# Two feed-forwards with the features of the product with w_ff1 on the partitions in seven of eight chunks

## The chip, the cores and the metric

The kernel runs on one core of a Trainium2 chip. The time is that of one execution on the device, in microseconds (us); the figure for a kernel is the median of its runs. Below, PE is TensorE (PEld its weight loads), DVE is VectorE, ACT is ScalarE, POOL is GpSimd and SP is SyncE, which issues the DMAs. "Span" is the time from the first profiled instruction of an execution to the end of the last.

## What is computed

Two transformer blocks in a row on 256 tokens of width 1024, in float32. What matters here is the feed-forward at the end of each, of width 4096 (`h` is the normalised input, (256, 1024)):

```python
# first block (pieces of hybrid_layer)
h2 = rmsnorm(x, g_ff_pre) * (1.0 + scale_f[:, None]) + shift_f[:, None]
y2 = jnp.square(jax.nn.relu(h2 @ w_ff1)) @ w_ff2
return x + gate_f[:, None] * rmsnorm(y2, g_ff_post)

# second block
h = rms_norm(x, pre_ffn_g[l])
f = jnp.square(jax.nn.relu(h @ w_ff1[l])) @ w_ff2[l]
x = x + rms_norm(f, post_ffn_g[l])
```

The rest (a gated mixer with attention, pooling and convolution in the first block; gating, attention, convolution and cross attention in the second) is as it was.

## The kernel before, in words

**Precision.** Every product is made of three matmuls in the type fp32r. A weight arrives as f32 (`raw`), ACT rounds it to `hi`, and DVE subtracts to get `lo` (`split_unit`, line 639). Activations are split in the same way (`evac_split`, line 728: ACT copies the high part, DVE subtracts for the low part). `mm3` (line 676) then adds high x high, low x high and high x low into one PSUM bank.

**Units.** Weights are loaded in units of 512 KB: two tiles of 128 rows by 512 columns. `w_ff1` and `w_ff2` have 32 units each, four to a chunk, in eight chunks of 512 features (`ffn`, line 1346). A unit takes three buffers of 128x1024 from a set of 36 (`k4`) while it is split, and two until PE has used it. A load is issued by SP when its buffer comes free.

**A chunk of the feed-forward, before.** Tokens stand on the partitions. For each of the two token tiles `t` of 128 tokens, PE holds a 128x128 tile of the transposed activations `xT[t]` as weights and moves 512 columns of `w_ff1` through: 4 units x 2 row tiles x 3 = 24 matmuls of 512 columns into the bank `f` (`chunk` and `use`, lines 833 and 681). Then `after` (line 1351): ACT takes the relu into `n` (`f1r` and `f2r` in the trace), PE transposes its four 128x128 tiles into another bank (`f1t`, `f2t`), ACT squares that (`f1s`, `f2s`), and `evac_split` makes high and low part of `r` (`f1rT`, `f2rT`), which stands with features on the partitions. The second product, with `w_ff2`, holds tiles of `r` as weights and moves 512 columns of `w_ff2`: 48 matmuls of 512 columns a chunk, added over all chunks in the four banks `y[t][i]`. The last chunk ends with `finish` for each token tile: in the first block that is `junction` (line 1369), which makes the input of the second block, in the second it writes the output.

**What feeds it.** In the first block `mixed` (line 1332) makes the activations with `norm_shift` (line 964): per token tile two halves of 512 columns, each transposed and split. In the second block `residual` and `junction` do it, quarter by quarter (`to_T_gain`). During the first chunks of the first feed-forward, DVE also adds up eight rows for the vector `GG2` (`mod_vector`), 512 KB each.

**Order.** The kernel records its operations first and plans them then. `schedule` (line 392) makes 30 passes over the list with its own costs, each pass with priorities from the one before, and takes the best. It sets the order on each engine and which buffer is used, so a change in one stage can give another order in stages behind it. An engine works in that order and waits where something is missing. Matmuls inside `rec.together()` stay together.

Of the kernel before, what the change touches and what calls it, by code (L numbers as in the profile page):

```python
# [19 lines left out]
P = 128  # L20
# [5 lines left out]
WHERE = {4: 0, 6: 1}  # L26

VERBOSE = 0
POOL_TAPS = 4
PASSES = 30  # L30
BOOST = 1.0
FADE = 0.7
# [8 lines left out]
NT = 2  # L41
# [108 lines left out]

class View:
# [57 lines left out]
class Wide:  # L209
# [367 lines left out]
def tile_two_blocks(ctx: ExitStack, tc: tile.TileContext, a: dict, out: bass.AP):  # L577
# [18 lines left out]
    def bank(name):  # L596
        return rec.tile([P, 512], "ps", name)
# [7 lines left out]
    def work(shape, tag, name, dt=F32):  # L605
        return rec.tile(shape, tag, name, dt)
# [226 lines left out]
    def chunk(wname, u0, nu, xT, name, n=512, after=None):  # L833

        us = [unit(wname, u0 + g) for g in range(nu)]
        ps = []
        for t in range(NT):
            o = bank(f"{name}{t}")
            for g in range(nu):
                use(us[g], xT[t], o[:, :n], g == 0, g == nu - 1)  # L840
            ps.append(o)
            if after:
                after(t, o)
        return ps
# [116 lines left out]
        sp.dma_start(xt, a["x"][t * P : (t + 1) * P, :])  # L961
        return xt

    def norm_shift(t, xG, r, S, name):

        hT = new_xT(f"{name}T{t}")
        for g, s in enumerate(H2):
            dve.scalar_tensor_tensor(xG[:, s], xG[:, s], r, S[:, s], op0=OP.mult, op1=OP.add)
            v = transposes(xG[:, s], 4, f"{name}{t}_t{g}")
            evac_split(hT[:, 0, 4 * g : 4 * g + 4, :], hT[:, 1, 4 * g : 4 * g + 4, :], v)  # L970
        return hT


    xrT = [work([P, 4, 256], "k4", f"xrT{h}") for h in range(2)]
# [352 lines left out]
        mT.append(m)  # L1327
    drain()
    GG1, G2, S2 = vec["GG1"], vec["G2"], vec["S2"]
    x1, hT = x0, []  # L1330

    def mixed(t, y):
        w = work([P, D], "k4", f"wG{t}")
        for s, yy in zip(H2, y):
            dve.tensor_mul(w[:, s], yy, GG1[:, s])
        r = rstd(squares(y, f"wo{t}"), f"wo{t}")
        for s in H2:
            dve.scalar_tensor_tensor(x0[t][:, s], w[:, s], r, x0[t][:, s], op0=OP.mult, op1=OP.add)
        r1 = rstd(squares([x0[t][:, s] for s in H2], f"x1{t}"), f"x1{t}")
        for s in H2:  # L1340
            dve.tensor_mul(w[:, s], x0[t][:, s], G2[:, s])
        hT.append(norm_shift(t, w, r1, S2, "h2"))

    proj("w_out", mT, "wo", mixed)

    def ffn(w1, w2, xT, name, finish):
        y = [[bank(f"{name}y{t}_{i}") for i in range(2)] for t in range(NT)]
        for c in range(8):
            rT = []

# [12 lines left out]
            for t in range(NT):
                for i in range(4):
                    use(us[i], None, y[t][i // 2], c == 0 and i % 2 == 0, c == 7 and i % 2 == 1, lambda k: (rT[t], k % 4))
                if c == 7:
                    finish(t, y[t])

    def junction(t, y, x, G, g, name):


        w = work([P, D], "k4", f"{name}w{t}")
        for s, yy in zip(H2, y):
            dve.tensor_mul(w[:, s], yy, G[:, s])
        r = rstd(squares(y, f"{name}y{t}"), f"{name}y{t}")
        hT = new_xT(f"{name}T{t}")
        for q in range(4):
            s = slice(256 * q, 256 * q + 256)
            dve.scalar_tensor_tensor(x[:, s], w[:, s], r, x[:, s], op0=OP.mult, op1=OP.add)
        to_T_gain(x, hT, g, f"{name}{t}")  # L1380
        rn = rstd(squares([x[:, s] for s in H2], f"{name}x{t}"), f"{name}x{t}")
        return hT, rn

    def residual(xs, G, g, name):
        hT, rs = [], []

        def after(t, y):
            h, r = junction(t, y, xs[t], G() if callable(G) else G, g, name)
            hT.append(h)
            rs.append(r)  # L1390

        return hT, rs, after
# [303 lines left out]
```

## Time and profile before

| | before |
|---|---|
| median of 3 runs | 812.25 us (810.99 to 816.01) |
| the profiled execution | 811.87 us, span 810.1 us |
| PE busy | 778.8 us (96%) |
| DVE busy | 583.3 us (72%) |
| ACT busy | 465.2 us (57%) |
| POOL busy | 87.8 us (11%) |
| DMA | 165.38 MB, 204 GB/s in the mean |
| granted PE clock, mean | 0.995 |

How to read it: busy time is the time in which an engine worked on at least one instruction. Matmuls are pipelined: one shows some 390 ns of duration while the next begins 227 ns after it, so the pace is read from starts, or from a piece of the chain with its count, not from the mean duration. The first feed-forward runs from some 256 to 446 us, the second from 620 us to the end.

### The profile page before, as it was taken

The numbers are of one execution on the slowest core, as the hardware profiler recorded it, in microseconds if no ns is written. First come the engines' busy times: TensorE is split into PE (matmuls) and PEld (weight loads), VectorE is DVE, ScalarE is ACT, GpSimd is POOL, SyncE is SP. The second block draws the span as 40 slices with busy tenths as digits, with TensorE's granted clock in tenths as the row PEclk, the third lists the DMA queues.
The fourth block names the chain that finished last, engine by engine and source line by source line (L and its number), as shares of the span: only waits on it lengthen the run. The fifth ranks groups of instructions, "written<-read, shape, count | busy, mean of one in ns | idle before, by whom it ended". The sixth has DMA issues, their size and how long they took to land.

```text
span 810.1 us, 10528 instructions
## 1 busy us (share of the span) xinstructions
PE 778.8 (96%) x3722; PEld 640.8 (79%) x3722; DVE 583.3 (72%) x908; ACT 465.2 (57%) x768; POOL 87.8 (11%) x133
## 2 busy tenths in 40 slices
PE   6999999999999999999999999789999999999996
PEld 4789888888877778888887887568888888888885
DVE  5998799998888985454537789999778744444513
ACT  6866665565266565455446764568567655454422
POOL 4301400004122000000000410103102100000000
PEclk9999999999999999999999999999999999999999
DMA  8999566578848775655656444033637655556501
GB/s 312 401 354 362 176 228 209 199 255 333 306 164 300 255 269 178 207 183 184 204 178 215 152 170 156 27 106 103 215 128 255 207 174 179 194 181 207 182 2 52
DMA packets 49629, 165.38 MB, mean 204 GB/s; under 512 B 5412, under 2 KB 6564, under 8 KB 49576
## 3 DMA queue, kind: packets, MB, share of 16 engines
q1 hardware_dynamic: 49576, 164.71, 58.6%
q8 instruction: 29, 0.48, 0.2%
q14 instruction: 24, 0.20, 0.1%
HBM read 163.64 MB, written 1.05 MB: 203 GB/s over the span
## 4 chain that ended last, share of the span: by engine, by line
PE 83%; DVE 7%; DMA 6%; ACT 2%; issue 1%; SPq 1%; DVEq 0%; POOLq 0%; ACTq 0%; POOL 0%
PE f2f L1645 11%; PE f2y L1645 11%; PE f1y L1645 10%; PE f1f L1645 9%; PE wo L1645 5%; PE kv L1645 3%; PE bcg L1645 3%; PE xq L1645 3%; PE bbg L1645 3%; PE xo L1645 3%; PE bag L1645 2%; DMA raw_w_xkv<-in_w_xkv_dram 2%; DVE dy L1645 2%; PE xA L1645 2%; PE aA L1645 1%; DMA raw_w_ff<-in_w_ff_dram 1%
## 5 line engine op out<-in xcount | busy, mean ns | idle before, releaser
L1645 DVE TENSOR_TENSOR lo_w_ff<-raw_w_ff,hi_w_ff 128x1024 fp32r<-128x1024 f32 x128 | 155.7, 1229 | 88.9 <-ACT hi_w_ff L1645 72.5
L1645 ACT ACTIVATE hi_w_ff<-raw_w_ff 128x1024 fp32r<-128x1024 f32 x128 | 132.8, 1056 | 83.0 <-DMA raw_w_ff<-in_w_ff_dram 70.3
L1645 DVE TENSOR_TENSOR lo_w_in<-raw_w_in,hi_w_in 128x1024 fp32r<-128x1024 f32 (+1 forms) x66 | 77.8, 1204 | 7.5 <-ACT hi_w_in L1645 6.8
L1645 PE MATMUL f1y<-hi_w_ff,f1rT 128*128 128x512 f32 x256 | 80.1, 393 | 0.2 <-DVE f1rT L1645 0.2
L1645 PE MATMUL f2f<-hi_w_ff,h5T 128*128 128x512 f32 x256 | 79.9, 393 | 0.0
L1645 PE MATMUL f2y<-hi_w_ff,f2rT 128*128 128x512 f32 x256 | 79.6, 392 | 0.0
L1645 PE MATMUL f1f<-hi_w_ff,h2T 128*128 128x512 f32 x256 | 79.6, 392 | 0.0
L1645 ACT ACTIVATE hi_w_in<-raw_w_in 128x1024 fp32r<-128x1024 f32 (+1 forms) x66 | 66.8, 1032 | 20.0 <-DMA raw_w_in<-in_w_in_dram 16.9
L1645 PEld LDWEIGHTS f2f<-hi_w_ff,h5T 128*128 128x128 f32 x256 | 47.5, 188 | 9.8 <-DVE h5T L1645 0.3
L1645 PEld LDWEIGHTS f1y<-hi_w_ff,f1rT 128*128 128x128 f32 x256 | 47.4, 188 | 10.0 <-DVE f1rT L1645 0.5
L1645 PEld LDWEIGHTS f1f<-hi_w_ff,h2T 128*128 128x128 f32 x256 | 47.6, 188 | 9.6
L1645 PEld LDWEIGHTS f2y<-hi_w_ff,f2rT 128*128 128x128 f32 x256 | 47.5, 188 | 9.4
L1645 PE MATMUL f1y<-lo_w_ff,f1rT 128*128 128x512 f32 x128 | 49.9, 390 | 0.0
L1645 PE MATMUL f2f<-lo_w_ff,h5T 128*128 128x512 f32 x128 | 49.9, 390 | 0.0
L1645 PE MATMUL f2y<-lo_w_ff,f2rT 128*128 128x512 f32 x128 | 49.9, 390 | 0.0
L1645 PE MATMUL f1f<-lo_w_ff,h2T 128*128 128x512 f32 x128 | 49.9, 390 | 0.0
L1645 PE MATMUL kv<-hi_w_xkv,memT 128*128 128x512 f32 x128 | 42.4, 412 | 6.2 <-ACT hi_w_xkv L1645 5.1
L1645 DVE TENSOR_TENSOR f1rT<-f1s,f1rT 128x512 fp32r<-128x512 f32 x16 | 11.1, 692 | 32.8 <-ACT f1rT L1645 32.8
L1645 PEld LDWEIGHTS kv<-hi_w_xkv,memT 128*128 128x128 f32 x128 | 24.4, 196 | 12.5 <-ACT hi_w_xkv L1645 5.5
L1645 DVE TENSOR_TENSOR f2rT<-f2s,f2rT 128x512 fp32r<-128x512 f32 x16 | 11.1, 692 | 30.4 <-ACT f2rT L1645 30.4
L1645 ACT ACTIVATE f2r<-f2f 128x512 f32<-128x512 f32 x16 | 9.6, 597 | 33.8 <-PE f2f L1645 33.8
L1645 PEld LDWEIGHTS f2y<-lo_w_ff,f2rT 128*128 128x128 f32 x128 | 24.0, 188 | 5.1
(461 smaller groups left out, 1729.4 us busy)
## 6 DMA issues: line engine op xcount, KB each, us to landing
raw_w_ff<-in_w_ff_dram SPq DMA_DIRECT2D x128, 512.0 KB, 3.6
raw_w_in<-in_w_in_dram SPq DMA_DIRECT2D x62, 512.0 KB, 4.6
raw_GG<-in_w_ada_dram SPq DMA_DIRECT2D x16, 512.0 KB, 5.5
raw_w_out<-in_w_out_dram SPq DMA_DIRECT2D x16, 512.0 KB, 5.2
raw_w_xkv<-in_w_xkv_dram SPq DMA_DIRECT2D x15, 512.0 KB, 9.2
G<-in_w_ada_dram SPq DMA_DIRECT2D x8, 512.0 KB, 8.1
S<-in_w_ada_dram SPq DMA_DIRECT2D x8, 512.0 KB, 9.7
raw_w_branch<-in_w_branch_dram SPq DMA_DIRECT2D x8, 512.0 KB, 4.6
```

Of the source, the lines that this page charges most:

```text
L1645: getattr(rec.real[op.eng], method)(*map(out_of, args), **{k: out_of(v) for k, v in kw.items()})
```

## The change

In chunk 0 of each feed-forward the way of before stays (`by_tokens`, the body of the old loop). Chunks 1 to 7 go through `by_features`. For each block `b` of 128 features out of the chunk's 512, PE now holds a 128x128 tile of `w_ff1` as weights, and moves activations: with the high part of the weights, both parts of all 256 tokens side by side (512 columns, into the whole bank), with the low part of the weights the high part of the activations alone (256 columns, into the bank's first half). That is 32 + 32 matmuls per chunk for the same three products. The result stands with features on the partitions. It is evacuated by block: ACT copies the bank's second half, DVE adds the first half to it, DVE takes relu and square at once (`max` and `mult`), ACT copies the high part, DVE subtracts for the low part.

For that, activations have another layout: four tiles `h2T` (or `h5T`), each with two row tiles, two parts and 256 tokens; the class `Fold` shows them to the token way as before. `rT` is laid out likewise: two tiles per chunk, each with two blocks and all 256 tokens, in place of one per token tile. `norm_shift` splits its halves in two steps of 256 columns, and so does chunk 0 with `rT`. `POOL_TAPS`, which is not used, goes. The core of the diff:

```diff
+class Fold:
+    def __init__(self, tiles, t):
+        self.tiles, self.s = tiles, slice(t * P, (t + 1) * P)
+
+    def __getitem__(self, k):
+        _, part, kt, _ = k
+        if isinstance(kt, int):
+            return self.tiles[kt // 2][:, kt % 2, part, self.s]
+        assert kt.stop - kt.start == 2 and kt.start % 2 == 0
+        return self.tiles[kt.start // 2][:, :, part, self.s]
...
+    def new_folded(name):
+        return [work([P, 2, 2, 256], "k4", f"{name}{i}", F32R) for i in range(4)]
...
-            evac_split(hT[:, 0, 4 * g : 4 * g + 4, :], hT[:, 1, 4 * g : 4 * g + 4, :], v)
+            for j in range(2):
+                k = slice(4 * g + 2 * j, 4 * g + 2 * j + 2)
+                evac_split(hT[:, 0, k, :], hT[:, 1, k, :], v[:, 2 * j : 2 * j + 2])
...
-                r = work([P, 2, 4, P], "k4", f"{name}rT{c}_{t}", F32R)
-                evac_split(r[:, 0], r[:, 1], sq)
-                rT.append(r)
-
-            chunk(w1, 4 * c, 4, xT, f"{name}f{c}_", after=after)
+                for i, r in enumerate(rT):
+                    v = Fold([r], t)
+                    evac_split(v[:, 0, 0:2, :], v[:, 1, 0:2, :], sq[:, 2 * i : 2 * i + 2])
+
+            chunk(w1, 4 * c, 4, [Fold(x, t) for t in range(NT)], f"{name}f{c}_", after=after)
+            return rT
+
+        def by_features(c):
+            rT = new_r(c)
+            us = [unit(w1, 4 * c + g) for g in range(4)]
+            for b in range(4):
+                ps = bank(f"{name}f{c}_{b}")
+                for g, (_, n, hi, lo) in enumerate(us):
+                    with rec.together():
+                        for j in range(2):
+                            s = slice(j * n + b * P, j * n + (b + 1) * P)
+                            xx = x[g][:, j]
+                            first, last = g == j == 0, g == 3 and j == 1
+                            both = dict(lhsT=hi[:, s], rhs=xx, start=first, stop=last)
+                            if first:
+                                pe.matmul(ps.cut(256), **both)
+                            pe.matmul(ps[:, :256], lhsT=lo[:, s], rhs=xx[:, 0], start=False, stop=False)
+                            if not first:
+                                pe.matmul(ps.cut(256), **both)
+                v = work([P, 256], "k1", f"{name}v{c}_{b}")
+                act.activation(v, ps[:, 256:], AF.Copy)
+                dve.tensor_tensor(v, ps[:, :256], v, op=OP.add)
+                sq = work([P, 256], "k1", f"{name}s{c}_{b}")
+                dve.scalar_tensor_tensor(sq, v, 0.0, v, op0=OP.max, op1=OP.mult)
+                r = rT[b // 2]
+                evac_split(r[:, b % 2, 0], r[:, b % 2, 1], sq)
+            return rT
+
+        for c in range(8):
+            rT = (by_features if c >= TOKENS_FIRST else by_tokens)(c)
...
-                    use(us[i], None, y[t][i // 2], c == 0 and i % 2 == 0, c == 7 and i % 2 == 1, lambda k: (rT[t], k % 4))
+                    use(us[i], None, y[t][i // 2], c == 0 and i % 2 == 0, c == 7 and i % 2 == 1, lambda k: (r, k % 4))
```

`TOKENS_FIRST` is 1. The order that the planner makes of it, in places that matter:

**PE, end of chunk 3 of the second feed-forward.** In a name, `f2f3_1` is the bank of the first product for chunk 3, `f2t3_1` its transposed relu, `f2y0_0` the bank `y[0][0]`, `w_ff1_215` and `w_ff2_212` are units 15 and 12, and the last number is a buffer's. Before, from the last matmuls of token tile 1 on:

```order
L1645 MATMUL f2f3_1_7081<-hi_w_ff1_215_6887,h5T11_6543 128x512
L1645 MATMUL f2f3_1_7081<-lo_w_ff1_215_6895,h5T10_6532 128x512
L1645 MATMUL f2y0_0_6607<-hi_w_ff2_212_6918,f2rT3_0_7115 128x512 x2
L1645 MATMUL f2y0_0_6607<-lo_w_ff2_212_6920,f2rT3_0_7115 128x512
L1645 MATMUL f2y0_0_6607<-hi_w_ff2_212_6918,f2rT3_0_7115 128x512 x2
L1645 MATMUL f2y0_0_6607<-lo_w_ff2_212_6920,f2rT3_0_7115 128x512
L1645 MATMUL f2t3_1_7146<-ident_402,f2r3_1_7140 128x128 x4
L1645 MATMUL f2y0_0_6607<-hi_w_ff2_213_6937,f2rT3_0_7115 128x512 x2
```

The transposes `f2t3_1` of tile 1 stand behind one group of six matmuls. After, the last matmuls of block 3, then the groups of the second product:

```order
L1701 MATMUL f2f3_3_7354<-h5T3_6610,lo_w_ff1_215_7125 128x256
L1701 MATMUL f2f3_3_7354<-h5T3_6610,hi_w_ff1_215_7112 128x512
L1701 MATMUL f2y0_0_6792<-hi_w_ff2_212_7165,f2rT3_0_7323 128x512 x2
L1701 MATMUL f2y0_0_6792<-lo_w_ff2_212_7169,f2rT3_0_7323 128x512
L1701 MATMUL f2y0_0_6792<-hi_w_ff2_212_7165,f2rT3_0_7323 128x512 x2
L1701 MATMUL f2y0_0_6792<-lo_w_ff2_212_7169,f2rT3_0_7323 128x512
L1701 MATMUL f2y0_1_6826<-hi_w_ff2_214_7226,f2rT3_0_7323 128x512 x2
L1701 MATMUL f2y0_1_6826<-lo_w_ff2_214_7228,f2rT3_0_7323 128x512
L1701 MATMUL f2y0_1_6826<-hi_w_ff2_214_7226,f2rT3_0_7323 128x512 x2
L1701 MATMUL f2y0_1_6826<-lo_w_ff2_214_7228,f2rT3_0_7323 128x512
L1701 MATMUL f2y0_0_6792<-hi_w_ff2_213_7177,f2rT3_1_7390 128x512 x2
```

No transposes are left; two groups of six, against blocks 0 and 1 (`f2rT3_0`), stand between block 3 and the first matmul that needs it (`f2rT3_1`). In eight of the fourteen changed chunks there are three such groups (also one for `f2y1_0`).

**DVE, the same chunk.** Before, from the last split ahead of the first subtraction to the one behind the second (`lo_w_ff2_216` is a weight split):

```order
L1645 TENSOR_TENSOR lo_w_ff2_217_7109<-raw_w_ff2_217_7092,hi_w_ff2_217_7107 128x1024
L1645 TENSOR_TENSOR f2rT3_0_7115<-f2s3_0_7113,f2rT3_0_7115 128x512
L1645 TENSOR_TENSOR lo_w_ff2_218_7142<-raw_w_ff2_218_7111,hi_w_ff2_218_7132 128x1024
L1645 TENSOR_TENSOR lo_w_ff2_219_7157<-raw_w_ff2_219_7130,hi_w_ff2_219_7144 128x1024
L1645 TENSOR_TENSOR f2rT3_1_7165<-f2s3_1_7163,f2rT3_1_7165 128x512
L1645 TENSOR_TENSOR lo_w_ff1_220_7190<-raw_w_ff1_220_7159,hi_w_ff1_220_7180 128x1024
```

After, from block 2 on (`f2v` is the sum of the two halves, `f2s` the square):

```order
L1701 TENSOR_TENSOR lo_w_ff2_216_7363<-raw_w_ff2_216_7303,hi_w_ff2_216_7359 128x1024
L1701 TENSOR_TENSOR f2v3_2_7361<-f2f3_2_7330,f2v3_2_7361 128x256
L1701 SCALAR_TENSOR_TENSOR f2s3_2_7380<-f2v3_2_7361 128x256
L1701 TENSOR_TENSOR lo_w_ff2_217_7388<-raw_w_ff2_217_7365,hi_w_ff2_217_7371 128x1024
L1701 TENSOR_TENSOR f2v3_3_7398<-f2f3_3_7354,f2v3_3_7398 128x256
L1701 SCALAR_TENSOR_TENSOR f2s3_3_7401<-f2v3_3_7398 128x256
L1701 TENSOR_TENSOR f2rT3_1_7390<-f2s3_2_7380,f2rT3_1_7390 128x256
L1701 TENSOR_TENSOR f2rT3_1_7390<-f2s3_3_7401,f2rT3_1_7390 128x256
L1701 TENSOR_TENSOR lo_w_ff2_218_7420<-raw_w_ff2_218_7378,hi_w_ff2_218_7418 128x1024
```

Two subtractions of 512 columns became four of 256, with four sums and four squares ahead of them; the weight splits of the next chunk stand between them as before.

**DVE, chunk 1 of the first feed-forward**, where the `GG2` rows stand too. Before:

```order
L1645 TENSOR_TENSOR lo_w_ff25_3298<-raw_w_ff25_3268,hi_w_ff25_3284 128x1024
L1645 SCALAR_TENSOR_TENSOR GG2_a_2933<-raw_GG2_5_3196,csil_409,GG2_a_2933 128x1024
L1645 TENSOR_TENSOR lo_w_ff26_3317<-raw_w_ff26_3280,hi_w_ff26_3309 128x1024
L1645 TENSOR_TENSOR lo_w_ff27_3329<-raw_w_ff27_3294,hi_w_ff27_3321 128x1024
L1645 SCALAR_TENSOR_TENSOR GG2_a_2933<-raw_GG2_6_3270,csil_409,GG2_a_2933 128x1024
L1645 SCALAR_TENSOR_TENSOR GG2_a_2933<-raw_GG2_7_3296,csil_409,GG2_a_2933 128x1024
L1645 TENSOR_TENSOR lo_w_ff18_3359<-raw_w_ff18_3306,hi_w_ff18_3340 128x1024
L1645 TENSOR_TENSOR f1rT1_0_3371<-f1s1_0_3369,f1rT1_0_3371 128x512
L1645 TENSOR_TENSOR GG2_lo0_3384<-GG2_a_2933,GG2_hi0_3379 128x512
```

After, from the same row's neighbourhood on:

```order
L1701 SCALAR_TENSOR_TENSOR GG2_a_2930<-raw_GG2_4_3194,csil_409,GG2_a_2930 128x1024
L1701 SCALAR_TENSOR_TENSOR GG2_a_2930<-raw_GG2_5_3215,csil_409,GG2_a_2930 128x1024
L1701 TENSOR_TENSOR lo_w_ff26_3333<-raw_w_ff26_3293,hi_w_ff26_3323 128x1024
L1701 TENSOR_TENSOR f1v1_0_3340<-f1f1_0_3313,f1v1_0_3340 128x256
L1701 SCALAR_TENSOR_TENSOR f1s1_0_3349<-f1v1_0_3340 128x256
L1701 TENSOR_TENSOR lo_w_ff25_3355<-raw_w_ff25_3278,hi_w_ff25_3296 128x1024
L1701 TENSOR_TENSOR f1rT1_0_3359<-f1s1_0_3349,f1rT1_0_3359 128x256
L1701 SCALAR_TENSOR_TENSOR GG2_a_2930<-raw_GG2_6_3280,csil_409,GG2_a_2930 128x1024
L1701 TENSOR_TENSOR f1v1_1_3376<-f1f1_1_3335,f1v1_1_3376 128x256
L1701 SCALAR_TENSOR_TENSOR f1s1_1_3387<-f1v1_1_3376 128x256
L1701 TENSOR_TENSOR lo_w_ff27_3393<-raw_w_ff27_3308,hi_w_ff27_3347 128x1024
L1701 TENSOR_TENSOR f1rT1_0_3359<-f1s1_1_3387,f1rT1_0_3359 128x256
```

The `GG2` rows and the splits of `w_ff2` (`lo_w_ff24` to `lo_w_ff27` are `w_ff2`'s units 4 to 7) now alternate with sums, squares and subtractions of chunk 1.

## Rows read from the trace of the kernel before

**Rows 1.** The page, part 1: span; busy us, share, instructions.

```profile
span 810.1 us, 10528 instructions
PE 778.8 (96%) x3722; PEld 640.8 (79%) x3722; DVE 583.3 (72%) x908; ACT 465.2 (57%) x768; POOL 87.8 (11%) x133
```

**Rows 2.** Busy time by stretch (us; its columns first).

```profile
core 0: us, PE busy (x) PEld busy (x) DVE busy (x) ACT busy (x) POOL busy (x), PEclk, DMA share, GB/s
256.00:300.00 44.00, 41.39 (x190) 33.20 (x189) 39.95 (x42) 28.27 (x39) 3.31 (x5) 1.00 0.75 270
300.00:420.00 120.00, 120.00 (x550) 99.36 (x550) 60.51 (x56) 61.14 (x73) 1.44 (x2) 1.00 0.55 184
480.00:545.00 65.00, 54.56 (x269) 42.02 (x268) 62.88 (x162) 36.82 (x89) 2.41 (x4) 0.97 0.30 98
630.00:800.00 170.00, 170.00 (x781) 140.79 (x780) 77.94 (x75) 81.67 (x104) 4.25 (x6) 1.00 0.48 158
```

**Rows 3.** Chain that ended last, second feed-forward: start us, us, what.

```profile
651.85 4.12 PE f2f L1645 x18
655.96 1.36 PE f2y L1645 x6
657.33 0.44 PE f2t L1645 x4
657.76 9.55 PE f2y L1645 x42
667.31 6.80 PE f2f L1645 x30
...
674.54 4.12 PE f2f L1645 x18
```

**Rows 4.** The same chain, in the first projection.

```profile
73.20 2.87 PE cc L1645 x24
```

**Rows 5.** Timeline, PE, second block: start us, us, instruction.

```profile
594.73 0.28 PE L1645 MATMUL xA<-lo_kx,xqT 128*128 128x256 f32 x1
594.85 0.63 PE L1645 MATMUL xo<-hi_w_xo,oxT 128*128 128x512 f32 x2
595.32 0.39 PE L1645 MATMUL xo<-lo_w_xo,oxT 128*128 128x512 f32 x1
...
604.17 0.39 PE L1645 MATMUL xo<-lo_w_xo,oxT 128*128 128x512 f32 x1
604.39 0.28 PE L1645 MATMUL xA<-xPT,hi_vx 128*128 128x256 f32 x1
```

**Rows 6.** Groups by form, ACT and DVE: busy us, mean ns, idle before.

```profile
L1645 ACT ACTIVATE hi_w_ff<-raw_w_ff 128x1024 fp32r<-128x1024 f32 x128 | 132.8, 1056 | 83.0 <-DMA raw_w_ff<-in_w_ff_dram 70.3
...
L1645 ACT ACTIVATE f2rT<-f2s 128x512 fp32r<-128x512 f32 x16 | 10.1, 632 | 0.5
L1645 ACT ACTIVATE f2r<-f2f 128x512 f32<-128x512 f32 x16 | 9.6, 597 | 33.8 <-PE f2f L1645 33.8
...
L1645 DVE TENSOR_TENSOR lo_w_ff<-raw_w_ff,hi_w_ff 128x1024 fp32r<-128x1024 f32 x128 | 155.7, 1229 | 88.9 <-ACT hi_w_ff L1645 72.5 <-PE f1y L1645 8.6 <-PE f2y L1645 7.2
L1645 DVE TENSOR_TENSOR f2rT<-f2s,f2rT 128x512 fp32r<-128x512 f32 x16 | 11.1, 692 | 30.4 <-ACT f2rT L1645 30.4
L1645 DVE TENSOR_TENSOR bPT<-bA,bPT 128x256 fp32r<-128x256 f32 x4 | 1.7, 418 | 0.1
```

**Rows 7.** Chain in chunk 1 of the first feed-forward.

```profile
288.38 1.06 ACT hi_w_ff L1645
289.44 0.49 ACT f1r L1645
289.93 0.04 issue
```

**Rows 8.** Waits of PE: us in total, times, longest.

```profile
PE f1t L1645 <- ACT f1r L1645: 3.5, 3, 1.3
```

**Rows 9.** Groups by form, weight loads: busy us, mean ns, idle before.

```profile
L1645 PEld LDWEIGHTS f2f<-hi_w_ff,h5T 128*128 128x128 f32 x256 | 47.5, 188 | 9.8 <-DVE h5T L1645 0.3
```

More of the change, by code (lines that the diff above doesn't have):

```diff
@@ L28 @@
 VERBOSE = 0
-POOL_TAPS = 4
+TOKENS_FIRST = 1
 PASSES = 30
@@ L962, in load_x, with norm_shift @@
         return xt
-    def norm_shift(t, xG, r, S, name):
-        hT = new_xT(f"{name}T{t}")
+    def norm_shift(t, xG, r, S, hT, name):
         for g, s in enumerate(H2):
@@ L969, in norm_shift @@
             v = transposes(xG[:, s], 4, f"{name}{t}_t{g}")
-            evac_split(hT[:, 0, 4 * g : 4 * g + 4, :], hT[:, 1, 4 * g : 4 * g + 4, :], v)
-        return hT
+            for j in range(2):
+                k = slice(4 * g + 2 * j, 4 * g + 2 * j + 2)
+                evac_split(hT[:, 0, k, :], hT[:, 1, k, :], v[:, 2 * j : 2 * j + 2])
     xrT = [work([P, 4, 256], "k4", f"xrT{h}") for h in range(2)]
@@ L1329, in tile_two_blocks @@
     GG1, G2, S2 = vec["GG1"], vec["G2"], vec["S2"]
-    x1, hT = x0, []
+    x1 = x0
+    h2 = new_folded("h2T")
     def mixed(t, y):
@@ L1341, in mixed, with ffn, new_r, by_tokens @@
             dve.tensor_mul(w[:, s], x0[t][:, s], G2[:, s])
-        hT.append(norm_shift(t, w, r1, S2, "h2"))
+        norm_shift(t, w, r1, S2, Fold(h2, t), "h2")
     proj("w_out", mT, "wo", mixed)
-    def ffn(w1, w2, xT, name, finish):
+    def ffn(w1, w2, x, name, finish):
         y = [[bank(f"{name}y{t}_{i}") for i in range(2)] for t in range(NT)]
-        for c in range(8):
-            rT = []
+        def new_r(c):
+            return [work([P, 2, 2, 256], "k4", f"{name}rT{c}_{i}", F32R) for i in range(2)]
+        def by_tokens(c):
+            rT = new_r(c)
             def after(t, ps):
@@ new lines, in by_tokens @@
+            return rT
+        def by_features(c):
+            rT = new_r(c)
+            us = [unit(w1, 4 * c + g) for g in range(4)]
[21 more added lines that the diff above has]
+            return rT
@@ L1362, in ffn @@
+        for c in range(8):
+            rT = (by_features if c >= TOKENS_FIRST else by_tokens)(c)
             us = [unit(w2, 4 * c + i) for i in range(4)]
             for t in range(NT):
+                r = Fold(rT, t)
                 for i in range(4):
-                    use(us[i], None, y[t][i // 2], c == 0 and i % 2 == 0, c == 7 and i % 2 == 1, lambda k: (rT[t], k % 4))
+                    use(us[i], None, y[t][i // 2], c == 0 and i % 2 == 0, c == 7 and i % 2 == 1, lambda k: (r, k % 4))
@@ L1366, in ffn, with junction @@
                 if c == 7:
                     finish(t, y[t])
-    def junction(t, y, x, G, g, name):
+    def junction(t, y, x, G, g, hT, name):
         w = work([P, D], "k4", f"{name}w{t}")
@@ L1375, in junction @@
         r = rstd(squares(y, f"{name}y{t}"), f"{name}y{t}")
-        hT = new_xT(f"{name}T{t}")
         for q in range(4):
@@ L1381, in junction, with residual @@
         rn = rstd(squares([x[:, s] for s in H2], f"{name}x{t}"), f"{name}x{t}")
-        return hT, rn
-    def residual(xs, G, g, name):
-        hT, rs = [], []
+        return rn
+    def residual(xs, G, g, name, folded=False):
+        rs = []
+        x = new_folded(f"{name}T") if folded else None
+        hT = [Fold(x, t) if folded else new_xT(f"{name}T{t}") for t in range(NT)]
         def after(t, y):
[L1388 to L1392, printed above, removed]
+            rs.append(junction(t, y, xs[t], G() if callable(G) else G, g, hT[t], name))
+        return x or hT, rs, after
     def scaled(r, fac, name, t):
@@ L1401, in tile_two_blocks @@
     hT3, r, after = residual(xs, lambda: vec["GG2"], "pre_mix_g_2", "h3")
-    ffn("w_ff1", "w_ff2", hT, "f1", after)
+    ffn("w_ff1", "w_ff2", h2, "f1", after)
     hT = hT3
@@ L1611, in tile_two_blocks @@
     G = load_gain(a["post_x_g_2"], "pxg")
-    hT, r, after = residual(xs, G, "pre_ffn_g_2", "h5")
+    h5, r, after = residual(xs, G, "pre_ffn_g_2", "h5", True)
     proj("w_xo_2", oxT, "xo", after)
@@ L1634, in finish @@
             sp.dma_start(out[t * P : (t + 1) * P, s], w[:, s])
-    ffn("w_ff1_2", "w_ff2_2", hT, "f2", finish)
+    ffn("w_ff1_2", "w_ff2_2", h5, "f2", finish)
     def out_of(v):
```

## The prediction

> **What bounds the kernel now.** I read the page's busy times first [rows 1]: TensorE (PE) is busy 778.8 us of a span of 810.1 us, VectorE (DVE) 72% and ScalarE (ACT) 57% of it. A mean over stages says little about one stage, so next come the stretches [rows 2]. From 300 to 420 us (the end of chunk 1 to that of chunk 6 of the first feed-forward, `f1`) and from 630 to 800 us (the second, `f2`) PE is busy in every microsecond, DVE in half of them (60.5 of 120, 77.9 of 170), DMA engines 0.48 to 0.55. These stages last as long as PE's instructions do, and the change is in them. PE idles in other places: 2.6 us between 256 and 300 us, where `f1` starts, and 10.4 us between 480 and 545 us, in the attention of the second block, where DVE is busy 62.9 us of 65.
>
> The third view is the chain of waits through one chunk of `f2` [rows 3]. The reader is to see there that the chain is PE alone, and that the pattern repeats: from 651.85 to 674.54 us is one chunk, 22.69 us. Its matmul pieces are 18, 6, 42 and 30 instructions in 4.12, 1.36, 9.55 and 6.80 us: 96 matmuls of 512 columns in 21.83 us, 0.2274 us each. The other two pieces are the eight transposes (`f2t`), 0.44 us for each four, 0.88 us a chunk. Half of the matmuls (48) are the product with `w_ff1`, half that with `w_ff2`.
>
> **The change on PE, per chunk.** It removes eight transposes, 0.88 us. The product with `w_ff1` had 48 matmuls of 512 columns (10.92 us). Now it has 4 blocks x 4 units x 2 = 32 wide ones (512 columns: the activations' high part beside their low part, against the weights' high part) and 32 narrow ones (256 columns, against the weights' low part). That is the same number of columns (24,576) with 16 more instructions, each with a weight load of its own. What a narrow one costs stands in the trace: 24 matmuls `cc` of 256 columns, each with its own load, take 2.87 us, 0.1196 us each [rows 4]. So the new product takes 32 x 0.2274 + 32 x 0.1196 = 11.10 us, where product and transposes took 10.92 + 0.88 = 11.80 us. The product with `w_ff2` keeps its 48 matmuls. A gain of 0.70 us a chunk, in 7 chunks of two feed-forwards: **14 x 0.70 = 9.8 us**.
>
> No row shows wide and narrow ones in turn; the places where one kind follows the other bound it [rows 5]. Behind a narrow one (594.73) the wide one starts 0.12 us later, and two wide ones take 0.47 us (594.85 to 595.32) instead of 2 x 0.2274 = 0.455: at worst 0.015 us more for each pair, 32 x 0.015 = 0.48 us a chunk, which leaves 0.22 us, 3.1 us in all. In front of a narrow one the wide one takes 0.22 us (604.17 to 604.39), which gives 0.007 back, and that is why I take the middle. At best a narrow one costs half a wide one, 0.1137 us: 0.19 us more a chunk, 12.4 us in all.
>
> A rule of the Trainium skill weighs against this. Its page "TensorE: Matmul & The Clock Gate", section "Back-to-back issue gap", says that in a sustained stream of load and matmul pairs 128 columns take some 81 ns and 512 some 131 ns, so that most of the price hangs on the instruction. An estimate from the page: 98 ns for 256 columns by the line through both, 48 x 131 + 8 x 81 = 6.9 us a chunk before and 32 x (131 + 98) = 7.3 us after, 0.4 us slower, some 817 us in all. The trace disagrees with its number: 227 ns at 512.
>
> **The change on the other engines.** In a chunk DVE had two subtractions of 512 columns (0.69 us each) beside eight weight splits; it gets four sums, four squares and four subtractions of 256: 4 x 3 x 0.42 = 5.0 us (the 256 columns of `bPT` give the 0.42), 3.6 us more. ACT had 2 x (0.60 + 0.60 + 0.63) = 3.7 us; it gets four copies from PSUM and four from SBUF. Their size is not in the rows: it lies between half of the price for 512 columns and the whole, 0.30 to 0.60 and 0.32 to 0.63 us. From 512 to 1024 columns 0.63 grows to 1.06, so half of 512 is 0.21 less: 0.39 and 0.42 us, 3.2 us a chunk [rows 6]. I cost both at nothing: PE's 22 us a chunk cover DVE's 8 x 1.23 + 5.0 = 14.8 us and ACT's 8 x 1.06 + 3.2 = 11.7 us.
>
> That cover is not enough by itself, because the second product waits for results. Behind the last matmul of block 3 stand copy, sum, square, copy and subtraction: 0.17 (a matmul's tail: 0.39 us long [rows 5], the next starts after 0.22) + 0.39 + 0.42 + 0.42 + 0.42 + 0.42 and five hand-overs of up to 0.04 us, like that between ACT and PE [rows 7], make 2.4 us. PE meanwhile has matmuls against blocks 0 and 1, in groups of six at 1.36 us. The order gives it two groups (2.7 us) in six of the chunks and three (4.1 us) in eight; in the latter a weight split stands between on DVE, 1.23 us. So 0.3 to 0.5 us are spare each time. A split on ACT that waits for its DMA, with block 3's copy queued behind it, would use that up, and PE would wait for it. It happens today: in [rows 7] the copy `f1r` of chunk 1 stands behind a split, and PE's transposes behind the copy. Three times PE waits so, 3.5 us in all, up to 1.3 us each [rows 8], out of 70 us that ACT waits for these DMAs [rows 6]. The first is in chunk 0, which keeps its transposes. The two in changed chunks (1 and 7) may vanish or turn into waits for `f1rT`.
>
> Chunk 1 of `f1` is the tightest. From 256 to 300 us DVE has 4.0 us free of 44 [rows 2], because it also adds up the eight `GG2` rows there, and the chunk's new evacuation takes 3.6 us more of it. The four units of `w_ff1` now all have to be split within the time of block 0 (11.1 / 4 = 2.8 us), where one token tile's half of the product left 5.5 us. So a pause of DVE becomes a pause of PE. I put the net of this place, of the two lost waits and of a few new ones at 0.5 us of loss, between 2.4 us of gain (both waits gone, DVE in time) and 2 us of loss (half of the 3.6 us).
>
> Chunk 0's finer pieces cost nothing: the last quarter of `h2T` is ready after 0.38 + 0.38 + 0.42 = 1.2 us, where a half took 0.60 + 0.69 = 1.3 us. SP issues the same DMAs, a few `GG2` rows two or three places later; slots, prefetch and end (the last 24 matmuls of one token tile, then the norm) keep their shape. Between 480 and 545 us the planner has put some PE and DVE work in another order; no view prices that, and I allow 2 us each way.
>
> **The sum.** The profiled execution took 811.87 us (0.4 us under the median of 812.25): 811.87 - 9.8 + 0.5 = 802.6 us.
>
> **The rivals.**
> - *The gain is eaten by waits for `f1rT` and `f2rT`.* For it: the 0.3 us spare in six chunks and ACT's 70 us behind DMAs. Against: today a transpose group of each chunk has 1.36 us of matmuls over a tail and a copy of 0.17 + 0.60 us, 0.6 us spare with splits ahead of it too, and `f2` shows no wait of PE from 630 to 800 us. Price: 1.1 us in each of the six, 6.6 us: 809 us.
> - *The gain goes to places that PE does not bound.* Chunk 1 runs at DVE's pace and the stretch from 480 to 545 us gets a worse order; 40 us of DVE in 44 speak for it, the fixed DVE work there against it. Some 5 us each: 812 us.
> - *Slower: the load of weights shows.* A load takes 188 ns by its row [rows 9]; if a narrow matmul could not hide it, the pair would take 0.2274 + 0.188 us, the product 13.29 us, 1.49 us more than today in each of 14 chunks: 833 us. It turns into a loss once a pair takes over 11.80 / 32 = 0.369 us, so 0.141 us for a narrow one. Against it: `cc` and `xA` hide theirs at 0.12 us.
> - *Slower: price by the instruction.* If each of the 16 added instructions cost a slot like a transpose's (0.11 us) on top of its columns, the chunk would lose 16 x 0.11 - 0.88 = 0.88 us: 824 us. Against: 0.1196 and 0.2274 us at 256 and 512 columns leave 12 ns for the instruction. The page named above says this with other figures.
>
> **Chances.** Forecast 0.68 (its own range 800 to 806 us), waits 0.17, gain lost elsewhere 0.09, load exposed 0.04, price by instruction 0.02. About 1% (8 us) is what a measurement of this kernel can tell from no change, so faster means under 804.1 us: four fifths of the forecast's chance, 0.55. Slower than 820.4 us are the last two, 0.06; the rest, 0.39, is within 1%. The range goes from 797 us (best narrow price, waits gone, a good order) to 810 us (the first rival with a little of the second); what it leaves out is the second rival and both slow ones, 0.15.
>
> **What would show it.** Right: f and y phases of 11.1 and 10.9 us in `f2`, a chunk in 22.0 us, PE without a pause from the first chunk to the end, 128x256 matmuls of `f2f` at a pitch of 0.12 us. Wrong: waits of PE `f2y` for DVE `f2rT` (first rival), more PE idle time between 270 and 300 or in the attention stretch (second), a pitch above 0.14 us (third). A chunk at 22.5 us would mean that the pair costs its upper bound.

## The result, and the profile after

| | before | after |
|---|---|---|
| median of 4 runs | 813.33 us (810.99 to 816.01) | 801.04 us (799.25 to 802.51) |
| ratio | | 0.985, 95% interval 0.9816 to 0.9884 |
| the profiled execution | 811.87 us, span 810.1 us | 800.44 us, span 798.7 us |

The kernel before has one run more here than in the table ahead of the prediction. The changed kernel is 1.5% faster. The profiled execution is 11.4 us shorter, where 9.8 - 0.5 = 9.3 us were forecast. The page's first part, span and busy time by engine, to set beside [rows 1]:

```profile
span 798.7 us, 10892 instructions
PE 768.4 (96%) x3834; PEld 640.3 (80%) x3834; DVE 628.6 (79%) x1056; ACT 459.9 (58%) x804; POOL 89.1 (11%) x133
```

PE does 10.4 us less with 112 instructions more; DVE does 45 us more. The stretches of [rows 2], of the changed kernel (the last ends where its second feed-forward does):

```profile
core 0: us, PE busy (x) PEld busy (x) DVE busy (x) ACT busy (x) POOL busy (x), PEclk, DMA share, GB/s
...
256.00:300.00 44.00, 42.71 (x212) 35.34 (x211) 41.83 (x56) 28.46 (x47) 3.08 (x5) 1.00 0.76 271
300.00:420.00 120.00, 120.00 (x612) 102.01 (x611) 80.45 (x110) 59.32 (x84) 1.29 (x1) 1.00 0.58 191
480.00:545.00 65.00, 53.28 (x260) 41.91 (x259) 62.86 (x159) 38.02 (x93) 3.57 (x8) 0.97 0.33 112
630.00:790.00 160.00, 160.00 (x810) 135.89 (x809) 96.23 (x139) 73.09 (x111) 0.94 (x3) 1.00 0.45 158
```

PE is still busy in every microsecond of the two long stretches, 300 to 420 and 630 to 790 us. DVE does 20 us more between 300 and 420 us, and only 2.2 of 44 us are free on it between 256 and 300; PE idles less there than before all the same (1.3 instead of 2.6 us). The chain that ended last, through one chunk and a half of the second feed-forward, which answers to [rows 3]:

```profile
637.62 11.18 PE f2f L1701 x64
648.80 10.88 PE f2y L1701 x48
659.68 11.18 PE f2f L1701 x64
```

A chunk goes from 637.62 to 659.68, 22.06 us, where it took 22.69. To see where the 11.4 us came from, both traces are cut at the same three places: the first matmul of the first feed-forward, its last one, and the first and last of the second. Before:

```profile
255.74:445.63 189.89, 185.97 (x852) 152.39 (x851) 115.41 (x117) 102.99 (x137) 5.77 (x11) 1.00 0.61 210
445.63:620.36 174.73, 163.89 (x826) 133.96 (x825) 152.57 (x328) 115.01 (x244) 26.66 (x44) 0.99 0.43 145
620.36:803.12 182.76, 182.74 (x841) 151.08 (x839) 89.07 (x96) 90.85 (x126) 7.49 (x11) 1.00 0.47 157
```

After (columns as above: stretch, its length, then PE busy):

```profile
255.43:438.25 182.82, 181.50 (x913) 152.53 (x912) 139.16 (x191) 101.42 (x155) 5.77 (x9) 1.00 0.65 218
438.25:613.12 174.87, 162.92 (x827) 134.27 (x825) 152.50 (x331) 114.89 (x246) 25.58 (x44) 0.99 0.43 144
613.12:791.70 178.58, 178.43 (x897) 150.79 (x895) 112.86 (x168) 87.78 (x142) 7.37 (x11) 1.00 0.46 162
```

The first feed-forward lost 7.07 us, the second 4.18, what lies between them gained 0.14. In the first, PE is busy 4.47 us less (185.97 to 181.50), which is about what the second gives too. The other 2.6 us are idle time of PE that is gone: 189.89 - 185.97 = 3.92 us before, 182.82 - 181.50 = 1.32 after. The waits of PE in the two feed-forwards after, to set beside [rows 8]:

```profile
PE f1t L1701 <- ACT f1r L1701: 0.7, 1, 0.7
...
PE h_t L1701 <- DVE wG L1701: 0.6, 1, 0.6
```

Both are at the start and in chunk 0, the one for the transposes that chunk 0 keeps. Before, the 3.5 us of [rows 8] were 1.1 in chunk 0, 1.1 in chunk 1 and 1.3 in chunk 7. No row has PE waiting for `f1rT` or `f2rT`.

### The profile page after: what moved, and what is told of

The parts are those of the page before. It is cut to its first block, busy times and chain, and to the rows that moved or that the text cites. A ratio compares the mean times of both kernels' runs of the same rounds, so it can differ in the third digit from the quotient of the medians.

```text
span 798.7 us, 10892 instructions
## 1 busy us (share of the span) xinstructions
PE 768.4 (96%) x3834; PEld 640.3 (80%) x3834; DVE 628.6 (79%) x1056; ACT 459.9 (58%) x804; POOL 89.1 (11%) x133
## 4 chain that ended last, share of the span: by engine, by line
PE 83%; DVE 6%; DMA 5%; ACT 3%; issue 1%; POOL 1%; SPq 1%; DVEq 0%; POOLq 0%; ACTq 0%
PE f1y L1701 11%; PE f2y L1701 11%; PE f2f L1701 10%; PE f1f L1701 10%; PE wo L1701 5%; PE kv L1701 3%; PE bcg L1701 3%; PE xq L1701 3%; PE bbg L1701 3%; DMA raw_w_xkv<-in_w_xkv_dram 2%; PE xo L1701 2%; DMA raw_w_out<-in_w_out_dram 2%; PE xA L1701 2%; DVE dy L1701 2%; PE aA L1701 1%; PE hb L1701 1%
## 5 line engine op out<-in xcount | busy, mean ns | idle before, releaser
L1701 ACT ACTIVATE hi_w_ff<-raw_w_ff 128x1024 fp32r<-128x1024 f32 x128 | 133.9, 1058 | 69.6 <-DMA raw_w_ff<-in_w_ff_dram 63.7
L1701 PE MATMUL f2f<-h5T,hi_w_ff 128*128 128x512 f32 x224 | 77.5, 396 | 0.0
L1701 PE MATMUL f1f<-h2T,hi_w_ff 128*128 128x512 f32 x224 | 77.5, 396 | 0.0
L1701 PE MATMUL f1f<-h2T,lo_w_ff 128*128 128x256 f32 x224 | 57.9, 279 | 0.0
L1701 PE MATMUL f2f<-h5T,lo_w_ff 128*128 128x256 f32 x224 | 57.9, 279 | 0.0
L1701 PEld LDWEIGHTS f2f<-h5T,hi_w_ff 128*128 128x128 f32 x224 | 40.5, 188 | 7.8
L1701 PEld LDWEIGHTS f1f<-h2T,hi_w_ff 128*128 128x128 f32 x224 | 40.5, 188 | 7.8
L1701 PEld LDWEIGHTS f2f<-h5T,lo_w_ff 128*128 128x128 f32 x224 | 42.2, 188 | 2.4
L1701 PEld LDWEIGHTS f1f<-h2T,lo_w_ff 128*128 128x128 f32 x224 | 42.2, 188 | 2.4
L1701 PEld LDWEIGHTS f1y<-lo_w_ff,f1rT 128*128 128x128 f32 x128 | 24.0, 188 | 5.0
## 6 DMA issues: line engine op xcount, KB each, us to landing
S<-in_w_ada_dram SPq DMA_DIRECT2D x8, 512.0 KB, 10.4
```

Of the source, the lines that this page charges most:

```text
L1701: getattr(rec.real[op.eng], method)(*map(out_of, args), **{k: out_of(v) for k, v in kw.items()})
```

## The experiments

All are made from the changed kernel if nothing else is said. Intervals are for the ratio to the kernel before, which ran beside each group of experiments (medians of 812.64 to 813.90 us).

**One at a time: first the arrangement of the data alone, then one feed-forward.** In the first, every chunk goes by tokens, so that only the layout of the activations, the finer splits and another plan are left.

```diff
-TOKENS_FIRST = 1
+TOKENS_FIRST = 8
```

> The new layout (four tiles of activations for both token tiles, two result tiles per chunk) stays, but all eight chunks go the token way, with transposes. Theory (the gain is PE's: 0.88 us of transposes less 0.25 us for the 16 added instructions a chunk, and the two lost waits of PE in the first feed-forward): the layout is worth nothing, 811 to 813 us, a chunk in 22.70 us, and one or two waits of PE for f1r after chunk 0. Rival (the new layout or the plan it leads to removes the waits): 809 to 810 us, no wait for f1r but that of chunk 0.

Measured: 811.24 us, ratio 0.9974 (0.9953 to 0.9995). The time is that of the theory, the waits lie between theory and rival:

```profile
PE f1t L1701 <- ACT f1r L1701: 1.1, 2, 0.7
...
PE f1y L1701 <- ACT f1rT L1701: 0.2, 1, 0.2
PE f1y L1701 <- DVE f1rT L1701: 0.2, 1, 0.2
```

Of the waits for the relu, 0.7 us are left in chunk 0 and 0.4 in chunk 1. That of chunk 7 is gone although its transposes are still there; 0.4 us for `f1rT` took its place. Next, the new product only in the first feed-forward, and only in the second:

```diff
-            rT = (by_features if c >= TOKENS_FIRST else by_tokens)(c)
+            rT = (by_features if c >= TOKENS_FIRST and name == "f1" else by_tokens)(c)
```

> Chunks 1 to 7 go by features in the first feed-forward alone, the second goes by tokens. Theory (waits of PE for f1r vanish because the first feed-forward's chunks have no transposes): 7 x 0.63 = 4.4 us plus 2.7 us of waits, 804.8 us. Rival (the 2.7 us come from somewhere else in the plan): 807.5 us.

> Chunks 1 to 7 go by features in the second feed-forward alone, the first goes by tokens. Theory: 7 x 0.63 = 4.4 us and nothing else, 807.5 us, with the waits of PE for f1r still there. Rival (the waits vanish through the layout or the plan): 804.8 us.

Measured: 805.47 us for the first feed-forward (0.9894, 0.985 to 0.9939), 807.62 for the second (0.9933, 0.991 to 0.9955), each nearer to its theory (804.8 and 807.5) than to its rival. Against the 811.24 of the arrangement alone these are gains of 5.8 and 3.6 us; their sum, 9.4, gives 801.8, and both together measured 801.0. So the new form itself brings 9.4 to 10.2 us by the medians; the intervals, some 2 us either way and more for the first feed-forward, are wider than the difference between these two figures. That the first feed-forward gains more than the second is not shown by the times, whose intervals overlap, but by the profiled executions, cut as above: the first takes 188.75 us by tokens alone and 182.55 with the new form, the second 183.03 and 178.56, which is 6.2 and 4.5 us less.

Where that surplus lies is seen in chunk 1 of the first feed-forward. The chain there, of the kernel by tokens alone, looks as in [rows 7]:

```profile
280.71 6.70 DMA raw_w_ff<-in_w_ff_dram
...
287.52 1.06 ACT hi_w_ff L1701
288.58 0.49 ACT f1r L1701
...
289.12 0.66 PE f1t L1701 x4
```

The same place with the new form in the second feed-forward alone has the same chain, 0.4 us later (`f1t` at 289.54), and PE waits 1.0 us there, beside 0.7 in chunk 0:

```profile
PE f1t L1701 <- ACT f1r L1701: 1.7, 2, 1.0
```

And in the changed kernel the chain is PE alone (`GG` is the vector product that follows from the `GG2` rows):

```profile
281.60 11.18 PE f1f L1701 x64
292.78 10.89 PE f1y L1701 x48
303.67 0.93 PE GG L1701 x4
```

ACT's split still waits for its DMA in that chunk, and the copies of block 2 and of `f1rT` stand behind it. The changed kernel's ACT there:

```profile
288.20 0.36 ACT L1701 ACTIVATE f1v<-f1f 128x256 f32<-128x256 f32 x1
289.79 1.06 ACT L1701 ACTIVATE hi_w_ff<-raw_w_ff 128x1024 fp32r<-128x1024 f32 x1 [1.23 <-DMA raw_w_ff<-in_w_ff_dram]
290.76 0.40 ACT L1701 ACTIVATE f1rT<-f1s 128x256 fp32r<-128x256 f32 x1
291.06 0.37 ACT L1701 ACTIVATE f1v<-f1f 128x256 f32<-128x256 f32 x1
```

PE does not notice: it has the next block's matmuls to do, and needs `f1rT` only at 292.78. Over the whole program ACT waits 63.7 us for these loads, 50 times (70.3 and 47 before). In the first feed-forward PE idles 3.9 us (before), 2.1 (by tokens alone) and 3.2 (second only) where tokens stand on the partitions; 1.3 (first only) and 1.3 (changed) where features do, by the same cuts. By tokens alone and second only have the first feed-forward in the same form, and differ by 1.1 us. The part of the 2.6 us that belongs to the new form is therefore 0.8 to 1.9 us; the rest came with the layout and the plan made for it, which the kernel by tokens alone has too, and these runs do not tell the two apart.

**Chunks 1 and 7 of the first feed-forward alone.** These are the two whose transposes waited.

```diff
-            rT = (by_features if c >= TOKENS_FIRST else by_tokens)(c)
+            rT = (by_features if name == "f1" and c in (1, 7) else by_tokens)(c)
```

> By features only in chunks 1 and 7 of the first feed-forward, those in which PE waited for f1r before; all others by tokens. Theory (each wait hung on the transposes of its own chunk): 2 x 0.63 + 2.3 = 3.6 us, 808.3 us, no wait of PE for f1r after chunk 0. Rival (the waits hang on late DMAs and go elsewhere, to f1r of other chunks or to f1rT): 810.5 us.

Measured: 810.23 us, 0.9967 (0.9947 to 0.9987). PE's waits:

```profile
PE f1t L1701 <- ACT f1r L1701: 0.7, 1, 0.7
```

One wait for the relu is left, that of chunk 0. The first feed-forward is 186.66 us long, 3.2 less than before: two chunks at 0.63, and some 2 us less idle time (3.9 to 1.8). But in the profiled execution 1.6 us more passed before its first matmul and 1.3 us more between the feed-forwards, at places that this edit does not touch by more than the plan. By its time the run looks like the rival, and by itself that decides nothing. Its waits are those of the theory, but most of this is not the edit's: the kernel by tokens alone, which has the same layout, idles 2.1 us in a first feed-forward of 188.75 us. Against it the two chunks bring 2.1 us, of which 0.3 is idle time. So what is shown is that chunk 1's wait goes with the transposes; that of chunk 7 had gone with the layout and the plan already.

**What the transposes cost.** The kernel before, with the transposes of the relu left out, so that the feed-forward squares an untransposed relu and its result is not the reference's:

```diff
-                tp = transposes(n, 4, f"{name}t{c}_{t}")
+                tp = n.cut(P)
```

> The kernel before, without the transposes of the relu in both feed-forwards: the square is taken from the untransposed relu, so the result of the feed-forward is left wrong on that account, and nothing is added in place of the transposes. Theory: 16 chunks x 0.88 us = 14.1 us less on PE, and PE's waits for f1r (3.5 us) may go as well or turn into waits for f1rT: 794.5 to 798 us. That the changed kernel gained 0.63 us a chunk and not 0.88 is then the price of the added instructions. Rival (PE's transposes were hidden behind something else): 808 us or more.

Measured: 796.26 us, 0.9784 (0.9746 to 0.9821). The chain in the second feed-forward:

```profile
658.35 10.88 PE f2f L1645 x48
669.23 10.88 PE f2y L1645 x48
```

A chunk takes 10.88 + 10.88 = 21.76 us, 0.93 less than the 22.69 of before. The transposes' own pieces in [rows 3] are 0.88 us; the remaining 0.05 lies in the matmuls behind them: the 18 behind one group of transposes took 4.12 us, 0.2289 each, and the 42 behind the other 9.55, 0.2274 each, where 48 in a row here take 10.88, 0.2267 each, as the 6 and the 30 ahead of transposes did. So the change could have brought 0.93 us a chunk at most, and brought 0.63: the narrow matmuls' price takes a third back. The waits go here too, in the old layout: PE has none for `f1r` or `f1rT`, and its idle time in the first feed-forward falls from 3.9 to 1.7 us (180.21 us long, 178.53 busy).

**Price by column or by instruction.** The narrow matmul is made as wide as the other one; it then also adds low x low, with the same number of instructions.

```diff
-                            pe.matmul(ps[:, :256], lhsT=lo[:, s], rhs=xx[:, 0], start=False, stop=False)
+                            pe.matmul(ps.cut(256), lhsT=lo[:, s], rhs=xx, start=False, stop=False)
```

> The changed kernel, with the low part of the weights against both parts of the activations too: the 448 narrow matmuls of 256 columns become 512 wide, the number of instructions and of weight loads stays (a fourth product, low x low, is added to the result). Price by the column: 32 x (0.2274 - 0.117) = 3.5 us a chunk, 14 x 3.5 = 49 us, 850 us. Price by the instruction or by the weight load: no change, 801 us; with 131 ns for 512 and 98 ns for 256 columns some 15 us, 816 us.

Measured: 849.64 us, 1.0445 (1.0405 to 1.0486), by column. A chunk in the first feed-forward:

```profile
335.15 14.51 PE f1f L1701 x64
349.66 10.88 PE f1y L1701 x48
```

64 matmuls of 512 columns take 14.51 us, 0.2267 each; with half of them narrow they take 11.18. Each 256 columns that were added cost (14.51 - 11.18) / 32 = 0.104 us. An instruction that has its price whatever its width (801 or 816 us) is out. So are the prediction's 824 us, by which each of the 16 added instructions costs 0.11 us on top of its columns: 64 matmuls in 11.18 us against 48 in 10.88 make 0.30 us for 16 of them, 0.02 each.

**Wide and narrow in groups.** If the change from one width to the other costs something, one wide matmul, eight narrow ones and then seven wide ones per block should be cheaper than the alternation. `wide(g, j)` is the wide matmul of unit `g`, row tile `j`, as it was.

```diff
...
+                with rec.together():
+                    wide(0, 0)
+                    for g, (_, n, hi, lo) in enumerate(us):
                         for j in range(2):
...
+                            pe.matmul(ps[:, :256], lhsT=lo[:, s], rhs=x[g][:, j][:, 0], start=False, stop=False)
+                with rec.together():
+                    for g in range(4):
+                        for j in range(2):
+                            if g or j:
+                                wide(g, j)
```

> The changed kernel with each block's matmuls in another sequence: one wide, eight narrow in a row, seven wide in a row, in place of wide and narrow in turn. Theory (each change between 512 and 256 columns costs some 1 to 2 ns, and the pair's 0.3494 us would be 0.2270 + 0.1195 in runs of one kind): 32 x 0.003 = 0.1 us a chunk, a piece of 11.09 us for 64 matmuls in place of 11.18, 1.2 us in all, 800 us. Rival (0.349 is what a narrow matmul beside its load costs in any sequence): 11.18 us, 801 us.

> The changed kernel as it is, on the same chip as the run with the other sequence, to compare with it: 801 us, a piece of 11.18 us.

Measured: 802.49 us grouped (0.9874, 0.9856 to 0.9893), 800.17 us for the changed kernel beside it on the same chip (0.9852, 0.9833 to 0.9872). No gain. The timeline of PE, alternating (the changed kernel):

```profile
660.69 0.40 PE L1701 MATMUL f2f<-h5T,hi_w_ff 128*128 128x512 f32 x1
660.93 0.28 PE L1701 MATMUL f2f<-h5T,lo_w_ff 128*128 128x256 f32 x1
661.04 0.40 PE L1701 MATMUL f2f<-h5T,hi_w_ff 128*128 128x512 f32 x1
```

Grouped:

```profile
662.48 2.00 PE L1705 MATMUL f2f<-h5T,hi_w_ff 128*128 128x512 f32 x8
664.32 1.11 PE L1705 MATMUL f2f<-h5T,lo_w_ff 128*128 128x256 f32 x8
665.27 2.00 PE L1705 MATMUL f2f<-h5T,hi_w_ff 128*128 128x512 f32 x8
```

Alternating, a pair takes 0.35 us (660.69 to 661.04, and 11.18 / 32 = 0.3494 over a chunk). Grouped, eight wide ones take 1.84 us and eight narrow ones 0.95, 2.79 for eight pairs, 0.349 each, and the chain's pieces are 11.17 us. The change of width costs nothing that grouping would save.

**A longer way from block 3 to the second product.** Four copies of 256 columns more on ACT, between the square and the split of block 3:

```diff
+                for i in range(4 if b == 3 else 0):
+                    u = work([P, 256], "k1", f"{name}u{c}_{i}")
+                    act.activation(u, sq, AF.Copy)
+                    sq = u
```

> The changed kernel, with four more copies of 256 columns on ACT in a row between square and split of block 3, some 1.7 us more between the last matmul of a chunk's first product and its last result (2.4 to 4.1 us). Theory (the second product has other groups of matmuls to put in front; the planner now puts four there, 5.4 us): no change, 800 to 802 us. Rival (the chain is at the edge of what PE can cover): 1 us or more in each of 14 chunks, 815 us.

Measured: 802.13 us, 0.9855 (0.9818 to 0.9892): no change. ACT and then DVE behind block 3 of a chunk of the second feed-forward:

```profile
672.29 0.38 ACT L1705 ACTIVATE f2v<-f2f 128x256 f32<-128x256 f32 x1 [0.33 <-PE f2f L1705]
673.63 0.42 ACT L1705 ACTIVATE f2u<-f2s 128x256 f32<-128x256 f32 x1 [0.95 <-DVE f2s L1705]
674.08 1.31 ACT L1705 ACTIVATE f2u<-f2u 128x256 f32<-128x256 f32 x3
675.43 0.42 ACT L1705 ACTIVATE f2rT<-f2u 128x256 fp32r<-128x256 f32 x1
```

```profile
675.88 0.43 DVE L1705 TENSOR_TENSOR f2rT<-f2u,f2rT 128x256 fp32r<-128x256 f32 x1 [1.95 <-ACT f2rT L1705]
```

The way is 1.8 us longer and ends at 676.31. The planner now puts four groups of six against blocks 0 and 1 first; they begin at 672.09 and last 4 x 1.36 = 5.44 us, to 677.53. So the rival with waits for `f2rT` needs more than 1.8 us to come true, not the 0.3 us that one order leaves, because the order is made anew. Four groups are all that stand against blocks 0 and 1, so a way that is more than some 3.0 us longer (an estimate, 5.44 - 2.4) would make PE wait; no run tried that.

**Chunk 0 as well.**

```diff
-TOKENS_FIRST = 1
+TOKENS_FIRST = 0
```

> Chunk 0 goes by features too, so that its first matmul needs both token tiles. Theory (the token way of chunk 0 covers the norm of the second token tile with 24 matmuls, 5.4 us): PE idles some 5.5 us more at the start of each feed-forward, less the 0.63 us that chunk 0 gains: 2 x 4.9 = 10 us, 811 us. Rival (something else covers it): 800 us.

Measured: 813.46 us, 0.9996 (0.9975 to 1.0017); the gain is gone. PE's waits:

```profile
PE h_t L1701 <- DVE wG L1701: 5.6, 1, 5.6
...
PE h_t L1701 <- DVE x0b L1701: 2.3, 1, 2.3
```

A block needs all 256 tokens, so it cannot start with the first token tile while the norm of the second is under way. In the profiled execution the first feed-forward starts at 264.35 instead of 255.43 us, and 184.0 instead of 174.9 us pass between the two; the feed-forwards themselves are only 2.9 and 0.6 us shorter. The token way of chunk 0 is what hides the second tile's norm.

The waits for it are 5.6 and 0.4 us at the first feed-forward, as forecast, but 2.3 and 0.8 at the second. They make half of the 18 us (8.9 and 9.1); another part is the granted clock. From 256.40 to 261.98 us PE does nothing, and from 262 to 266 the granted clock is 0.50, the lower of its two levels (1.2 GHz); from 268 it is 1.00 again. The two stretches from the first feed-forward on:

```profile
264.35:444.23 179.88, 179.88 (x907) 152.52 (x908) 132.57 (x185) 93.10 (x140) 3.71 (x4) 0.99 0.61 211
444.23:628.23 184.00, 168.60 (x834) 137.73 (x832) 156.74 (x334) 119.09 (x256) 28.20 (x47) 0.96 0.41 142
```

Between the feed-forwards PE idles 3.5 us more than in the changed kernel (15.4 against 11.9) and is busy 5.7 us longer with 7 matmuls more, at a clock of 0.96 against 0.99. The clock is lowest from 520 to 545 us, in the attention, at 0.77; the changed kernel shows 0.91 from 494 to 514 us and 1.00 from 514 to 539. This edit reaches that place by the plan alone. All eight runs have a mean clock of 0.981 to 0.990, the four of the changed kernel 0.993 to 0.998. So the 811 us of the expectation came out near the measured time partly by luck.

## Why the prediction was right

The forecast was 802.6 us, in a range of 797 to 810; the median is 801.04. The profiled execution, on which the sum was made, came to 800.44, 2.2 us under the sum. The steps one by one:

- **PE bounds both feed-forwards.** Right: busy 120 of 120 and 160 of 160 us after the change too.
- **0.70 us a chunk.** Right in kind, a little too much: a chunk takes 11.18 + 10.88 = 22.06 us, 0.63 less than 22.69, which makes 14 x 0.63 = 8.8 us instead of 9.8. The term that was mis-sized is the pair: 0.3494 us, where 0.2274 + 0.1196 = 0.3470 were put in (32 x 0.0024 = 0.08 us a chunk). The upper bound from the timeline, 0.015 us more a pair, was six times too wide. The product with `w_ff2` became 0.03 us cheaper than its 10.91, since no transposes stand in it.
- **The rule that spoke against it.** By column, the traces say: 0.2267 us at 512 columns and 0.12 at 256, and 48.6 us more when the narrow ones are widened. By the rule of the Trainium skill, "TensorE: Matmul & The Clock Gate", section "Back-to-back issue gap", which has 131 ns at 512 columns and 81 ns at 128, the change would have been a loss of 0.4 us a chunk, an estimate. These runs do not agree with it for fp32r at a granted clock of 1.00; the trace's own row was the better guide.
- **DVE and ACT are covered.** Right. The groups by form, after:

```profile
L1701 DVE TENSOR_TENSOR f2rT<-f2s,f2rT 128x256 fp32r<-128x256 f32 x32 | 13.4, 422 | 7.8 <-ACT f2rT L1701 6.8
L1701 ACT ACTIVATE f2rT<-f2s 128x256 fp32r<-128x256 f32 x32 | 13.1, 417 | 22.3 <-DVE f2s L1701 22.3
...
L1701 ACT ACTIVATE f2v<-f2f 128x256 f32<-128x256 f32 x28 | 10.8, 385 | 27.4 <-PE f2f L1701 26.7
```

  0.42 and 0.39 us for ACT's halves, as worked out from 0.63 and 1.06.
- **The way behind block 3.** Right almost to the hundredth. In the chunk whose block 3 ends at 648.64, DVE's last rows are

```profile
649.25 0.42 DVE L1701 TENSOR_TENSOR f2v<-f2f,f2v 128x256 f32<-128x256 f32 x1
649.71 0.42 DVE L1701 SCALAR_TENSOR_TENSOR f2s<-f2v 128x256 f32<-128x256 f32 x1
650.06 0.99 DVE L1701 TENSOR_TENSOR f2rT<-f2s,f2rT 128x256 fp32r<-128x256 f32 x2
```

  so `f2rT` is there at 651.05, 2.41 us after 648.64 (2.4 forecast). Two groups of six end at 648.64 + 2.72 = 651.36: 0.3 us spare, and no wait.
- **0.5 us of loss in chunk 1 and the waits.** This is the step that failed, by its size and its sign: PE idles 2.6 us less, just outside the bound of 2.4 that was given for "both waits gone, DVE in time". Both of these happened. Only 0.8 to 1.9 us of it belong to the new form; the rest came with the layout and its plan, for which the prediction had no term. For the form's part, the mistake was to weigh the 4.0 us that DVE had free there as if PE would feel each delay of DVE: in the new form a late copy holds up one block's result, which PE needs several microseconds later, where before a late relu held up the transposes that were next in PE's order. In the changed kernel's chunk 1 a split on ACT still waits 1.23 us for its DMA, and PE does not stop.
- **The stretch between the feed-forwards.** Allowed 2 us each way; 0.14.

The sum with what was measured: 811.87 - 8.8 - 2.6 = 800.5, beside 800.44. The forecast had 1.0 us too much for the chunks and 3.1 us too little for the waits; that these stand against each other brought it within 2.2 us, and this much is luck. The rivals: waits for `f1rT` and `f2rT` appear in no row of the changed kernel; the gain was not lost elsewhere; a narrow matmul hides its load of 188 ns as `cc` does.

## What to carry to other kernels

Where PE bounds a stage, add up its matmuls, each at the price that its width has in the kernel's own rows: here 0.23 us at 512 columns, 0.12 at 256 and 0.11 for a transpose of 128. Swapping the operands so that the result comes out in the orientation that the next product needs removed eight transposes a chunk and left the number of columns in the product as it was, for 16 more instructions at 0.02 us each. A form in which PE does not need its neighbour's result at once can save idle time beside its own instructions: 0.8 to 1.9 us here, beside 8.8. The form that needs all tokens at once must not be the first after a norm that delivers them tile by tile; as first chunk of both feed-forwards it cost 12 us, a part of it by a lower granted clock.

## What was not expected of the hardware

Two widths in turn cost 0.3494 us a pair, 0.0024 over the sum of the two prices that the rows of before give, and grouping does not bring that back. Behind a group of transposes the wide matmuls are dearer than among themselves, 0.03 to 0.04 us for each group, so leaving eight transposes out brought 0.93 us a chunk, where their own pieces are 0.88.
